# Running maxima of the mLSTM gates: 32 rows at once instead of eight times 4 rows

## The chip, the core and the metric

The kernel runs on one core of a Trainium2 chip. The metric is the device time of one execution in microseconds. Before the change three runs gave 2087.04, 2087.28 and 2087.66 us; their median, 2087.28, is the time before. Engines are named as in the profile: PE is the matrix engine (TensorE), PEld its weight load, DVE the vector engine, ACT the scalar engine, POOL GpSimd, SP the engine whose queue issues most DMAs.

## The reference

One encoder layer over two sequences of 512 tokens (`x_prompt`, `x_sample`) with 1024 channels, in float32: a half-step SwiGLU feed-forward block, a mixing block, a second feed-forward block, a final RMS norm. The mixing block runs attention and a bidirectional mLSTM next to each other on one input projection. The change concerns the mLSTM's stabilisers. Per head (4) and direction (2):

```python
b = jnp.cumsum(lf, axis=-1)                       # lf: log forget gate, within a chunk
D = b[..., :, None] - b[..., None, :] + li[..., None, :]
D = jnp.where(tril, D, -jnp.inf)
inter = b + m[..., None]
m_t = jnp.maximum(inter, jnp.max(D, axis=-1))
...
S_qk = jnp.einsum('bhtd,bhsd->bhts', qc, kc) * jnp.exp(D - m_t[..., None])
...
g = bL[..., None] - b + li
m_new = jnp.maximum(bL + m, jnp.max(g, axis=-1))
```

Since `b_t` does not depend on `s`, the maximum over the row is `b_t` plus a running maximum over `s` of `li_s - b_s`. The second direction is the same on the flipped sequence.

## The kernel before, in words

Tokens are handled in four blocks of 128; the kernel uses these blocks as chunks of the mLSTM, where the reference has 64; the stabilised sums are the same, grouped otherwise. Float32 products are made of three products of split operands (high times high, high times low, low times high), so each projection is a long row of 128 x 128 by 128 x 512 matmuls (L755 for a projection of 128 channels, L739 for one by tokens).

The two sequences go through the generator `mix(s, ...)`, which is advanced in turns: the first sequence (`s` = 0) computes its gates while its own projections run; the second computes them while the output projection of the first (`out_unit`, L1212) is still running, whose squares POOL adds up (L156) and whose result POOL's queue writes (L1213). The order of instructions on each engine is set by a scheduler from priorities, dependences and its own costs; each engine then works through its list in order, and SP through its DMAs in order.

`gates()` turns the gate columns into log gates of shape 128 tokens x 32, where the 32 columns are direction, block and head (`d b h`); one matmul group (L900) makes the cumulative sums `cs`, and `et` (L903) holds the gate exponents, input gate minus cumulative forget gate. What is needed from `et` is its running maximum along the tokens of each block, forward for direction 0 and backward for direction 1, and the exponents as rows in DRAM (`ebuf`). As tokens lie on partitions, the kernel turns `et` first. For each direction:

- four turns on PE (L907), one per block, give 4 rows (heads) of 512 tokens in one PSUM bank;
- DVE copies them to `er` (L909), SP writes them to `ebuf` (L910);
- `mem_max` makes four scans on DVE (L869), one per block, of 4 rows x 128 tokens each;
- for each block PE turns the running maxima back (L874) and the block's last maximum, broadcast over 128 columns (L875); DVE copies both to `st` (L876).

That is 24 turns, 8 scans, 2 copies to `er`, 2 DMAs and 2 copies to `st` per sequence. Around them on PE stand the products of a projection (L755), the turns of the keys (`k_turn`, L847) whose banks ACT empties (L849), and later the turns of the rotated queries (`q_rope`, L960). On DVE stand the sums of squares of the queries (`ssq`, L785), a reciprocal square root (L162 to L192), the rotation of the queries (L796 to L807) and the splitting of weights (L240).

`mem_scales` (L989 to L1000) reads `st` and makes the stabilisers. It is issued in the program after the attention heads, but the scheduler may place it earlier. `mem_rows(h, d)` reads a row of `ebuf`, 512 tokens of one head, broadcast to all 128 partitions (L979), and adds a mask (L983, POOL for the first sequence, DVE for the second); `mem_head` makes the decay weights from them on ACT. PSUM banks for turns come from a pool of two (`PT`), those for scores likewise (`PS`).

Of the kernel before, what the change touches and what calls it, by code (L numbers as in the profile page):

```python
# [8 lines left out]
F32 = mybir.dt.float32  # L9
# [3 lines left out]
ALU = mybir.AluOpType  # L13
AX = mybir.AxisListType
PSUM = bass.MemoryType.PSUM

P = 128
S = 512
# [8 lines left out]
def encoder(ctx, tc, I, outs):  # L27
    nc = tc.nc
    cpool = ctx.enter_context(tc.tile_pool(name="cpool", bufs=1))
    dpool = ctx.enter_context(tc.tile_pool(name="dpool", bufs=1, space=bass.MemoryType.DRAM))  # L30
# [11 lines left out]
    def nm(s):  # L42
        n_id[0] += 1
        return f"{s}_{n_id[0]}"
# [71 lines left out]
    def PT():  # L116
        return pt.tile([P, S], F32, tag="t", name=nm("pst"))
# [8 lines left out]
    ident = cpool.tile([P, P], F32, name="ident")  # L126
# [140 lines left out]
    V_ = nc.vector  # L267
# [394 lines left out]
    HM, DM = 4, 128  # L662
    NEG = -1e30
# [96 lines left out]
    def mix(s, xh, xl, early=None, extra=None, after=None):  # L760
# [8 lines left out]
        def F2(dtype=F32):  # L769
            return T2(dtype, "f2")  # L770
# [81 lines left out]
        def gs(tag):  # L852
            t = small(32, tag)
            return t, t.rearrange("p (d b h) -> p d b h", d=2, b=4)

        cs = small(96, "cs")
        csv = cs.rearrange("p (j d b h) -> p j d b h", j=3, d=2, b=4)
        ebuf = dpool.tile([2, 4, S], F32, name=nm("ebuf"))

        st = spool.tile([P, 4, 2, 4, HM], F32, tag="st", bufs=1, name=nm("st"))  # L860
        n1, bd, en, n2 = [st[:, i] for i in range(4)]

        def mem_max(d, er):

            run = F2()[0:4]
            for b in range(4):
                bs = slice(b * P, (b + 1) * P)
                to, x_ = [t[:, bs] if d == 0 else t[:, bs][:, ::-1] for t in (run, er[0:4])]
                V_.tensor_tensor_scan(to, x_, x_, NEG, op0=ALU.max, op1=ALU.max)  # L869
            p = PT()  # L870
            pv = p[:, 0:32].rearrange("p (i b h) -> p i b h", i=2, b=4)
            for b in range(4):
                end = b * P + (P - 1 if d == 0 else 0)
                nc.tensor.transpose(pv[:, 0, b], run[:, b * P:(b + 1) * P], ident[0:4, 0:4])  # L874
                nc.tensor.transpose(pv[:, 1, b], run[:, end:end + 1].to_broadcast([4, P]), ident[0:4, 0:4])  # L875
            V_.tensor_copy(st[:, 0:2, d], pv)  # L876

        def gates():
            Gb = Gt.rearrange("p (b c) -> p b c", b=4)
# [16 lines left out]
            p = PT()  # L896
# [4 lines left out]
            V_.tensor_copy(cs, p[:, 0:96])  # L901
            et, ev = gs("et")
            V_.tensor_tensor(et, Is, cs[:, 32:64], op=ALU.add)  # L903
            for d in range(2):
                p = PT()
                for b in range(4):
                    nc.tensor.transpose(p[0:4, b * P:(b + 1) * P], ev[:, d, b, :], ident)  # L907
                er = F2()
                V_.tensor_copy(er[0:4], p[0:4])  # L909
                nc.sync.dma_start(ebuf[d], er[0:4])  # L910
                mem_max(d, er)


        Vm = []
# [61 lines left out]
        def mem_rows(h, d):  # L976

            eb = T2(F32, "eb")
            nc.sync.dma_start(eb, ebuf[d, h:h + 1, :].rearrange("a s -> (a s)").partition_broadcast(P))  # L979
            em = T2(F32, "eb")  # L980
            eb3 = eb.rearrange("p (b s) -> p b s", b=4)
            em3 = em.rearrange("p (b s) -> p b s", b=4)
            (G_, V_)[s].tensor_tensor(em3, eb3, tabs[3][:, d].unsqueeze(1).to_broadcast([P, 4, P]), op=ALU.add)  # L983
            return eb3, em3
# [258 lines left out]
    def turn(s, k, bank):  # L1243
        p = bank()
        for b in range(4):
            nc.tensor.transpose(p[:, b * P:(b + 1) * P], raws[s][:, b, k * P:(k + 1) * P], ident)
        return p
# [58 lines left out]
    for k in range(HK_):  # L1306
        x1l, x1u = x1[2 * k % 4], x1[(2 * k + 1) % 4]
        for t, kk, bank, kr in ((x1l, k, PS, orow[3]), (x1u, k + HK_, PT, orow[4])):
            p = turn(1, kk, bank)
# [220 lines left out]
```

## Time and profile before

| | |
|---|---|
| median of three runs | 2087.28 us (2087.04 to 2087.66) |
| profiled execution, its own time | 2087.16 us |
| its span in the trace | 2085.4 us, 27317 instructions |
| PE busy | 2065.5 us, 9520 matmuls and turns |
| DVE busy | 1558.2 us |
| ACT busy | 894.3 us |
| POOL busy | 95.6 us |
| DMA | 454.33 MB, 218 GB/s on average |
| granted clock of PE | 0.998 |

The span is what the trace covers; 1.8 us of the execution lie around it. Rows of the trace name the line of the kernel before, the engine, and the tile written and read (`out<-in`). A row of the timeline gives start, length, engine, line, operation, tiles, shape and count. Since matmuls overlap, a row's length is longer than what the instruction adds to the queue; the distance between starts tells that.

### The profile page before, as it was taken

The page shows a single profiled execution, that of the slowest core. Times are in us where ns is not written, and L with a number is a line of the kernel's source. Part 1 is how long each engine was busy: PE and PEld are TensorE (multiplying, and loading weights), DVE is VectorE, ACT ScalarE, POOL GpSimd, SP SyncE. Part 2 cuts the span into 40 slices and gives each one's busy share as a digit, 9 for nine tenths or more (in the row PEclk, how much of TensorE's full clock was granted, in tenths as well). Part 3 has the DMA queues.
Part 4 walks back from the last instruction along what each step waited for, and adds up shares of the span by engine and source line. Part 5 has one row for each costly group of instructions (what it writes and reads, how often), then busy time and mean ns, then how long its engine had stood idle before and what let it go on. Part 6 is the DMA issues. An engine that isn't in the chain of part 4 may idle for free.

```text
span 2085.4 us, 27317 instructions
## 1 busy us (share of the span) xinstructions
PE 2065.5 (99%) x9520; PEld 1694.8 (81%) x9520; DVE 1558.2 (75%) x2850; ACT 894.3 (43%) x1645; POOL 95.6 (5%) x114
## 2 busy tenths in 40 slices
PE   8999999999999999999999999999999999999998
PEld 6888888888888777888878788888888888888887
DVE  7888888786797897675577645545888888795797
ACT  6544444443234566463344443323544444442222
POOL 1000000001003000100120000002000000000010
PEclk9999999999999999999999999999999999999999
DMA  8655555699766655777675345677656555599853
GB/s 279 204 173 193 192 172 182 205 342 359 259 225 242 202 162 172 257 241 270 214 263 180 103 152 182 203 255 245 205 172 212 185 178 182 180 347 346 274 190 116
DMA packets 300857, 454.33 MB, mean 218 GB/s; under 512 B 20048, under 2 KB 170592, under 8 KB 299696
## 3 DMA queue, kind: packets, MB, share of 16 engines
q1 hardware_dynamic: 298848, 447.13, 63.9%
q0 software_dynamic: 1872, 5.46, 0.8%
q8 instruction: 75, 1.23, 0.2%
q14 instruction: 62, 0.51, 0.1%
HBM read 285.63 MB, written 166.89 MB: 217 GB/s over the span
## 4 chain that ended last, share of the span: by engine, by line
PE 94%; DMA 2%; DVE 2%; ACT 1%; issue 0%; SPq 0%; DVEq 0%; ACTq 0%; POOL 0%
PE mm L755 21%; PE pss L333 17%; PE pst L333 11%; PE mm L333 9%; PE mm L589 9%; PE pst L589 4%; PE pss L589 4%; PE mm L739 4%; PE pso L589 3%; PE pso L1039 1%; PE pss L1012 1%; PE pso L739 1%; PE pst L1031 1%; DMA wr<-in_ffn_w_gate_dram 1%; PE pso L1175 1%; PE pst L755 1%
## 5 line engine op out<-in xcount | busy, mean ns | idle before, releaser
L755 PE MATMUL mm<-xh,w 128*128 128x512 f32 x896 | 291.2, 394 | 0.0
L333 PE MATMUL pss<-xc,w 128*128 128x512 f32 x1056 | 256.3, 391 | 0.7 <-DVE t L364 0.7
L333 PE MATMUL mm<-xc,w 128*128 128x512 f32 x1056 | 253.0, 390 | 2.4 <-ACT w L291 1.9
L333 PE MATMUL pst<-xc,w 128*128 128x512 f32 x1056 | 253.7, 389 | 0.0
L333 PEld LDWEIGHTS pss<-xc,w 128*128 128x128 f32 x1056 | 196.9, 188 | 47.9 <-DVE t L364 7.3
L333 PEld LDWEIGHTS mm<-xc,w 128*128 128x128 f32 x1056 | 197.3, 188 | 45.0 <-ACT w L291 2.8
L333 PEld LDWEIGHTS pst<-xc,w 128*128 128x128 f32 x1056 | 198.1, 188 | 41.4 <-ACT t L368 0.2
L755 PEld LDWEIGHTS mm<-xh,w 128*128 128x128 f32 x896 | 167.7, 188 | 33.6
L589 PE MATMUL mm<-rt,w 128*128 128x512 f32 (+1 forms) x819 | 188.4, 384 | 0.0
L755 PE MATMUL mm<-xl,w 128*128 128x512 f32 x448 | 176.7, 394 | 0.0
L589 PEld LDWEIGHTS mm<-rt,w 128*128 128x128 f32 x819 | 151.3, 188 | 29.8
L291 ACT ACTIVATE w<-t 128x512 fp32r<-128x512 f32 x176 | 106.9, 627 | 139.1 <-issue 55.2
L292 DVE TENSOR_TENSOR w<-t,w 128x512 fp32r<-128x512 f32 x176 | 118.2, 688 | 54.2 <-ACT w L291 52.3
L333 PE MATMUL pss<-xc,f 128*128 128x512 f32 x528 | 126.9, 389 | 0.0
L333 PEld LDWEIGHTS pss<-xc,f 128*128 128x128 f32 x528 | 99.1, 188 | 20.6
L657 ACT ACTIVATE w<-wr 128x512 fp32r<-128x512 f32 x72 | 45.1, 632 | 138.3 <-PE pso L589 70.8
L657 ACT ACTIVATE w<-t 128x512 fp32r<-128x512 f32 x82 | 51.8, 632 | 107.6 <-PE pst L589 62.4
L755 PEld LDWEIGHTS mm<-xl,w 128*128 128x128 f32 x448 | 84.3, 188 | 16.6
L589 PE MATMUL pst<-rt,w 128*128 128x512 f32 x396 | 93.7, 389 | 0.0
L589 PE MATMUL pss<-rt,w 128*128 128x512 f32 x396 | 93.7, 389 | 0.0
L239 ACT ACTIVATE w<-wr 128x1024 fp32r<-128x1024 f32 (+1 forms) x56 | 57.2, 1028 | 71.3 <-PE mm L755 29.8
L589 PEld LDWEIGHTS pss<-rt,w 128*128 128x128 f32 x396 | 74.3, 188 | 15.4
(341 smaller groups left out, 3657.8 us busy)
## 6 DMA issues: line engine op xcount, KB each, us to landing
rt<-rbuf SPq DMA_DIRECT2D x154, 512.0 KB, 5.7
wpark<-w SPq DMA_DIRECT2D x104, 512.0 KB, 3.5
w<-wpark SPq DMA_DIRECT2D x104, 512.0 KB, 4.6
wr<-in_ffn_w_gate_dram SPq DMA_DIRECT2D x62, 512.0 KB, 5.3
rbuf<-tab SPq DMA_DIRECT2D x102, 256.0 KB, 3.8
wr<-in_ffn_w_up_dram SPq DMA_DIRECT2D x44, 512.0 KB, 4.5
rbuf<-f SPq DMA_DIRECT2D x72, 256.0 KB, 3.9
wr<-in_w_in_dram SPq DMA_DIRECT2D x36, 512.0 KB, 6.0
```

Source lines behind the costliest of these rows:

```text
L239: pin(nc.scalar.activation(hi, raw, AF.Copy))
L291: pin(nc.scalar.activation(t[:, 0], src, AF.Copy))
L292: pin(V_.tensor_tensor(t[:, 1], src, f(t[:, 0]), op=ALU.subtract))
L333: nc.tensor.matmul(p, a[:, k, :], xt[:, b, k, :], start=(first and k == 0 and i == 0), stop=(k == HK_ - 1 and i == 2), skip_group_check=True)
L589: nc.tensor.matmul(p, u[:, a, d * P:(d + 1) * P], r[:, b, ts], start=(first and q == 0 and k == 0), stop=(q == len(us) - 1 and k == 2), sk ...
L657: nc.scalar.activation(hi, src, AF.Copy)
L739: nc.tensor.matmul(p[b][:, :N], a[:, k, bs], w_[:, kl, :], start=(k == 0 and i == 0), stop=(k == KD - 1 and i == 2))
L755: nc.tensor.matmul(p, a[:, k, :], b, start=(k == 0 and i == 0), stop=(k == n - 1 and i == 2))
L1012: nc.tensor.matmul(p, qT[:, h, b * P:(b + 1) * P], kv[:, hk * 2 + j, :], start=(j == 0), stop=(j == 1))
L1031: nc.tensor.transpose(p[:, b * P:(b + 1) * P], Ps[b][:, kb * P:(kb + 1) * P], ident)
L1039: nc.tensor.matmul(po, Vst[:, kv_, hk, :], w, start=(kv_ == 0 and i == 0), stop=(kv_ == 3 and i == 1))
L1175: nc.tensor.matmul(po, vm[:, a, t, hs_], b, start=(t == 0 and n == 0), stop=(t == 3 and n == 2))
```

## The change

All 32 rows (direction, block, head) are handled together. One turn takes `et` as a whole (128 x 32) to 32 rows of 128 tokens. One copy and one DMA bring them to `er` and `ebuf`, which now is laid out as direction, block, head, token. One scan runs backward over all 32 rows and then a second forward over the first 16, direction 0, overwriting them. The block's last maximum is the maximum of the row, made by one reduction (`top`). Two turns, of the running maxima and of `top` broadcast over 128 columns, and one copy fill `st`. Per sequence these are 3 turns, 2 scans, 1 reduction, 2 copies and 1 DMA. `mem_rows` reads the row of a head as four pieces of 128 tokens, one for each block, because in the new layout the blocks of a head lie apart.

```diff
--- before.py
+++ after.py
@@ -855,25 +855,9 @@
 
         cs = small(96, "cs")
         csv = cs.rearrange("p (j d b h) -> p j d b h", j=3, d=2, b=4)
-        ebuf = dpool.tile([2, 4, S], F32, name=nm("ebuf"))
-
+        ebuf = dpool.tile([2, 4, HM, P], F32, name=nm("ebuf"))
         st = spool.tile([P, 4, 2, 4, HM], F32, tag="st", bufs=1, name=nm("st"))
         n1, bd, en, n2 = [st[:, i] for i in range(4)]
-
-        def mem_max(d, er):
-
-            run = F2()[0:4]
-            for b in range(4):
-                bs = slice(b * P, (b + 1) * P)
-                to, x_ = [t[:, bs] if d == 0 else t[:, bs][:, ::-1] for t in (run, er[0:4])]
-                V_.tensor_tensor_scan(to, x_, x_, NEG, op0=ALU.max, op1=ALU.max)
-            p = PT()
-            pv = p[:, 0:32].rearrange("p (i b h) -> p i b h", i=2, b=4)
-            for b in range(4):
-                end = b * P + (P - 1 if d == 0 else 0)
-                nc.tensor.transpose(pv[:, 0, b], run[:, b * P:(b + 1) * P], ident[0:4, 0:4])
-                nc.tensor.transpose(pv[:, 1, b], run[:, end:end + 1].to_broadcast([4, P]), ident[0:4, 0:4])
-            V_.tensor_copy(st[:, 0:2, d], pv)
 
         def gates():
             Gb = Gt.rearrange("p (b c) -> p b c", b=4)
@@ -901,14 +885,20 @@
             V_.tensor_copy(cs, p[:, 0:96])
             et, ev = gs("et")
             V_.tensor_tensor(et, Is, cs[:, 32:64], op=ALU.add)
-            for d in range(2):
-                p = PT()
-                for b in range(4):
-                    nc.tensor.transpose(p[0:4, b * P:(b + 1) * P], ev[:, d, b, :], ident)
-                er = F2()
-                V_.tensor_copy(er[0:4], p[0:4])
-                nc.sync.dma_start(ebuf[d], er[0:4])
-                mem_max(d, er)
+            p = PT()
+            nc.tensor.transpose(p[0:32, 0:P], et, ident)
+            rows = F2()[0:32]
+            er, run = rows[:, 0:P], rows[:, P:2 * P]
+            V_.tensor_copy(er, p[0:32, 0:P])
+            nc.sync.dma_start(ebuf.rearrange("d b h s -> (d b h) s"), er)
+            V_.tensor_tensor_scan(run[:, ::-1], er[:, ::-1], er[:, ::-1], NEG, op0=ALU.max, op1=ALU.max)
+            V_.tensor_tensor_scan(run[0:16], er[0:16], er[0:16], NEG, op0=ALU.max, op1=ALU.max)
+            top = rows[:, 2 * P:2 * P + 1]
+            V_.tensor_reduce(top, er, axis=AX.X, op=ALU.max)
+            p = PT()
+            nc.tensor.transpose(p[:, 0:32], run, ident[0:32, 0:32])
+            nc.tensor.transpose(p[:, 32:64], top.to_broadcast([32, P]), ident[0:32, 0:32])
+            V_.tensor_copy(st[:, 0:2], p[:, 0:64].rearrange("p (i d b h) -> p i d b h", i=2, d=2, b=4))
 
 
         Vm = []
@@ -976,9 +966,9 @@
         def mem_rows(h, d):
 
             eb = T2(F32, "eb")
-            nc.sync.dma_start(eb, ebuf[d, h:h + 1, :].rearrange("a s -> (a s)").partition_broadcast(P))
+            eb3 = eb.rearrange("p (b s) -> p b s", b=4)
+            nc.sync.dma_start(eb3, ebuf[d, :, h, :].partition_broadcast(P))
             em = T2(F32, "eb")
-            eb3 = eb.rearrange("p (b s) -> p b s", b=4)
             em3 = em.rearrange("p (b s) -> p b s", b=4)
             (G_, V_)[s].tensor_tensor(em3, eb3, tabs[3][:, d].unsqueeze(1).to_broadcast([P, 4, P]), op=ALU.add)
             return eb3, em3
```

## The prediction

> **What bounds the kernel now.** I read the page first, then the waits of TensorE (PE), the windows around the two gate computations, and the timelines of both.
>
> ```profile
> span 2085.4 us, 27317 instructions
> PE 2065.5 (99%) x9520; PEld 1694.8 (81%) x9520; DVE 1558.2 (75%) x2850; ACT 894.3 (43%) x1645; POOL 95.6 (5%) x114
> PE 94%; DMA 2%; DVE 2%; ACT 1%; issue 0%; SPq 0%; DVEq 0%; ACTq 0%; POOL 0%
> PE pst L874 <- DVE f L869: 1.0, 1, 1.0
> ```
>
> PE is busy for 2065.5 of 2085.4 us and makes 94% of the chain that ended last (third line). The last line is from PE's waits (total us, times, longest): beyond the start of the program, the one wait of a microsecond belongs to the code that changes, a transpose (L874) that waits for a running maximum (L869). So the kernel ends when PE has worked through its queue, and every PE instruction taken out should show in the time unless it uncovers a wait.
>
> ```profile
> 690.00:706.00 16.00, 15.98 (x93) 12.09 (x92) 10.99 (x38) 7.52 (x14) 0.00 (x0) 1.00 0.38 103
> 706.00:720.00 14.00, 14.00 (x75) 11.53 (x74) 13.94 (x31) 8.34 (x17) 0.00 (x0) 1.00 0.69 225
> 1066.00:1080.00 14.00, 14.00 (x77) 11.44 (x76) 13.78 (x33) 8.33 (x18) 1.10 (x2) 1.00 0.89 296
> 1080.00:1110.00 30.00, 30.00 (x138) 24.78 (x137) 11.62 (x14) 7.71 (x13) 8.69 (x9) 1.00 0.95 343
> ```
>
> Columns: stretch, length, busy time of PE, PEld, DVE, ACT, POOL, granted clock, DMA share, GB/s. The first sequence's gates lie in 690 to 706: PE is never free there, the clock is full, POOL is idle. Just behind the gates of either sequence DVE (VectorE) is as full as PE (13.94 and 13.78 of 14), so DVE work that goes is useful too, but alone it would not show.
>
> **The turns that go.** First sequence: from the first turn of `et` to the steady product stream behind the gates.
>
> ```profile
> 694.65 0.60 PE L907 MATMUL pst<-ident,et 128*4 128x128 f32 x4
> 705.09 0.70 PE L755 MATMUL mm<-xh,w 128*128 128x512 f32 x2
> ...
> L755 PE MATMUL mm<-xh,w 128*128 128x512 f32 x14 | 4.8, 412 | 0.0
> L755 PE MATMUL mm<-xl,w 128*128 128x512 f32 x7 | 3.0, 433 | 0.0
> L847 PE MATMUL pst<-ident,qT 128*128 128x128 f32 x16 | 2.8, 286 | 0.0
> ...
> 703.55 0.87 PE pst L847 x8
> 705.33 3.90 PE mm L755 x17
> ```
>
> Two timeline rows, then the groups between them, then two pieces of the chain. Durations of single matmuls overlap, so I price by the chain: an undisturbed product takes 3.90/17 = 0.229 us, a full turn 0.87/8 = 0.109. The stretch is 705.09 - 694.65 = 10.44 us and holds 21 products and 16 other turns: 10.44 - 21 x 0.229 - 16 x 0.109 = 3.89 us are the 24 turns of the gates. Eight of these are L907, 0.87 us by the price of a full turn; the other eight pairs (L874 with L875) then cost 3.02/8 = 0.38 us each: narrow turns between wide products slow their neighbours.
>
> Second sequence, likewise:
>
> ```profile
> 1055.52 0.60 PE L907 MATMUL pst<-ident,et 128*4 128x128 f32 x4
> 1057.80 0.39 PE L755 MATMUL mm<-mh,w 128*128 128x512 f32 x1
> 1059.16 0.19 PE L874 MATMUL pst<-ident,f 4*128 4x4 f32 x1 [0.97 <-DVE f L869]
> 1066.42 0.38 PE L847 MATMUL pst<-ident,qT 128*128 128x128 f32 x2
> ...
> L755 PE MATMUL mm<-mh,w 128*128 128x512 f32 x15 | 5.2, 411 | 0.0
> L755 PE MATMUL mm<-ml,w 128*128 128x512 f32 x7 | 2.8, 402 | 0.0
> L847 PE MATMUL pst<-ident,qT 128*128 128x128 f32 x12 | 2.1, 286 | 0.0
> ```
>
> 10.90 - 22 x 0.229 - 12 x 0.109 = 4.55 us. Of that, 1059.16 - 1057.80 - 0.23 = 1.13 us is the wait for the scan; 3.42 us are turns, 0.32 a pair.
>
> The changed kernel has one L907-like turn and one pair. Turns of 32 rows do not occur in this trace; the bounds are a full turn, 0.11, and the pair of 4 rows, 0.38; I take 0.11 plus one pair, 0.49 and 0.43. Removed: 3.40 + 2.99 = 6.39 us. If the three cost as little as full turns, 0.2 more goes.
>
> **What PE waits for then, first sequence.** The order listing of the changed kernel puts eight products between the turn of `et` and the turn of the running maxima, where ten stood. Eight products end at about 694.65 + 0.11 + 8 x 0.229 = 696.6. On DVE the chain is copy, a `ssq` reduction that the scheduler put between, scan, reduction, scan.
>
> ```profile
> 693.59 0.26 DVE L901 COPY cs<-pst 128x96 f32<-128x96 f32 x1 [1.21 <-PE pst L900]
> 694.53 0.68 DVE L785 TENSOR_REDUCE ssq<-t 128x8 f32<-128x512 f32 x1
> 696.49 0.40 DVE L869 TENSOR_TENSOR_SCAN f<-f 4x128 f32<-4x128 f32 x1
> 696.82 0.14 DVE L162 TENSOR_SCALAR rs<-ssq 128x32 f32<-128x32 f32 x1
> ```
>
> The copy of 128 columns is priced by L901 (96 columns, 0.26): 0.29, 0.2 until the next can start. A scan has 0.40 and lets the next start after 0.33; 32 partitions instead of 4 with the same 128 columns should cost the same (eight 128-column scans become two, so at most this doubles to 0.8 each; nothing shows that). The reduction of 128 columns is a quarter of L785, 0.2 to 0.3. One turn lasts 0.27 (0.60 for four, less three starts of 0.109), so the copy starts at 694.96, and 0.22 + 0.60 + 0.33 + 0.20 + 0.40 brings the last scan's end to 696.7. PE follows a scan by some 0.15 (worked out from the next rows): 696.85, a new wait of 0.2. At double scans it is 0.9. Behind the DVE copy, which now waits for a turn that has just been issued, stand the `ssq` reduction and the rest of DVE's queue; this idles DVE 0.35 us, covered by its 5 us of free time in 690 to 706.
>
> **The second sequence: a shared wait.**
>
> ```profile
> L869 DVE TENSOR_TENSOR_SCAN f<-f x16: 385/404/1489, 696.5 to 1062.7; 4x128 f32<-4x128 f32 x16
> 1056.32 0.67 DVE L909 COPY f<-pst 4x512 f32<-4x512 f32 x1
> 1056.92 0.67 DVE L796 TENSOR_TENSOR t<-t,rs 128x512 f32<-128x512 f32 x1
> 1057.52 2.43 DVE L869 TENSOR_TENSOR_SCAN f<-f 4x128 f32<-4x128 f32 x4
> 1056.71 0.54 POOL L1213 DMA_DIRECT2D x2buf<-f  x1 [6.23 <-DVE f L1212]
> 1057.27 1.47 POOL L156 TENSOR_TENSOR R<-R,t 128x512 f32<-128x512 f32 x1
> ```
>
> One scan of 16 took 1489 ns instead of 404: the first of the second sequence, from 1057.52 to 1059.01. POOL's add ran from 1057.27 to 1058.74; the scan finished 0.27 after it. That is what PE waited for: it went on at 1059.16, 0.15 behind the scan. The Trainium skill (SBUF — State Buffer, "Who interferes with whom") says that a DVE instruction with two SBUF inputs and a GpSimd instruction that reads SBUF exclude each other for the whole instruction, and that a reduction does not take part; by that rule, with which this row agrees, the second of the two new scans can be caught as the first was.
>
> In the changed order the copy (now L909, 0.60 from its start to that of L796) takes 0.22, so L796 starts at about 1056.54 and the first scan 0.60 later at 1057.14, 0.13 before POOL's add, which follows POOL's transfer issue of 1056.71. Either the scan is first, POOL starts at 1057.5 and the second scan waits until about 1058.9 and ends at 1059.15; or the first scan is caught, ends at 1059.0 as now, and the second at 1059.6. PE gets on at 1059.3 or 1059.75. Its ten products end at about 1058.0 in both kernels. So the wait is 1.3 or 1.75, I take 1.45, where it was 1.13: 0.3 lost. At best, if no scan is caught, it is 0.2 and 0.9 is won; at worst a second add of POOL follows, 1.3 more. Behind a caught scan stand the steps of the query rotation on DVE; PE asks for their turns some 3.5 us later (16 turns and six products), which covers it.
>
> **What else moves.** The `kv` turns (L847) now stand in one block, each needing a bank that ACT or DVE has just emptied; PE may stand 0.15 us per sequence there, 0.3 in all. The small steps of `mem_scales` move ahead of the query rotation in the first sequence; DVE has 14 instructions fewer in all, 2 x (2 x 0.68 + 8 x 0.40) = 9.1 us of copies and scans give way to about 2.8, so the rotation still starts earlier by as much as PE does. On ACT the exponential of `mem_scales` now stands before the fourth `kv` copy and waits for DVE; the bank that this holds is asked for only some 29 products later. On SP two `ebuf` writes become one; in the second sequence a weight load that stood behind the later of them is issued earlier. The sixteen `mem_rows` loads read four pieces of 512 bytes per partition instead of one of 2 KB: taken at nothing, with their price among the rivals.
>
> **Sum**, against the profiled execution's own time of 2087.16 us (span 2085.4 and 1.8 around it; the three runs' median is 2087.28): -6.39 + 0.2 + 0.3 + 0.3 = -5.6, so 2081.6 us. The bounds make it 2081.0 (cheap turns, the short wait, no stand at the `kv` turns) to 2083.2 (double scans, the long wait, 0.6 at the `kv` turns). A change of 0.2%, 4.2 us, is about what a measurement of this kernel can tell from no change.
>
> **Rivals.**
>
> A. No scan meets POOL: the wait of 1.13 shrinks to 0.2 instead of growing to 1.45, 1.25 better than the sum, 2080.3 us. For it: the scan leads POOL's add by an estimated 0.13 us; against it: the second scan starts well inside the add. 16%.
>
> B. Part of the gain is lost in the score stage. From about 730 us on, the order listing shows scores, turns and products of the first sequence interleaved anew, and DVE is full there (13.94 of 14 before it). If PE waits for bank after bank on DVE, I price it at half of what is removed from the first sequence's DVE and PE queues, 2 to 3 us: 2084.1. Against it: DVE's work shrinks by as much as PE's. 15%.
>
> C. The loads of `mem_rows` land late, and the kernel is slower.
>
> ```profile
> box<-ebuf SPq DMA_DIRECT2D x16, 256.0 KB, 4.6
>   DVE box L983: 12.8, 6
> wr<-in_w_in_dram SPq DMA_DIRECT2D x36, 512.0 KB, 6.0
> 1107.52 0.69 DVE L983 TENSOR_TENSOR box<-box,tab 128x512 f32<-128x512 f32 x1 [2.77 <-DMA box<-ebuf]
> 1109.50 0.69 DVE L937 TENSOR_TENSOR f<-mm,R 128x512 f32<-128x512 f32 x1 [0.69 <-PE mm L755]
> ```
>
> In the second sequence DVE itself waits for such a load (2.77 us at 1107.52), with the query split and the score maxima queued behind it; 0.69 us of slack stand at L937. Eight loads of that sequence feed DVE; if the six for which DVE waited (second row: 12.8 us in six waits) land x later, PE loses up to 6 (x - 0.7). It outweighs the gain by 0.2% from 6 (x - 0.7) = 5.6 + 4.2, x = 2.3 us; at 3 us later the time is 2081.6 + 13.8 = 2095. Against it: a weight load of twice the bytes, also in pieces of 512 bytes (128 columns), lands in 6.0, so x should be below 1.4. The Trainium skill (DMA: Bandwidth & Descriptors, "Specifications") puts the least piece for full rate at 512 bytes, which these just meet; by that rule x is near nothing. 5%.
>
> D. PE's gain is given back at the next supply limit: in 1080 to 1110 DMA stands at 0.95 and 343 GB/s, and weights that land when they land hold PE at the old time. 2086.5. Against it: PE is busy for 30.00 of the 30 us there, so no weight came late. 6%.
>
> The forecast keeps 58%. That the edit does not do what it says is no rival: the order listing shows 3 gate turns a sequence for 24, and DVE's 14 instructions fewer.
>
> **Chances.** Faster by over 0.2%: forecast and A, 74%. Within 0.2% (above 2083.0): B and D, 21%. Slower: C, 5%. The range 2079.6 to 2084.4 holds the forecast, A and most of B.
>
> **What would show it.** Right: L907, L874 and L875 replaced by three turns a sequence; PE's waits show one wait of 1.2 to 1.8 us for a scan near 1054 (both stretches lie about 3 us earlier by then) and about 0.2 near 697; one long scan; the span 5 to 6 us shorter, nearly all of it before 1070. Wrong: a `box<-ebuf` landing above 7 us with DVE waiting behind it, PE waits for `asm` or `pss` after 720, or a turn of 32 rows that costs several tenths.

## The result and the profile after

The changed kernel takes 2084.39 us (median of 20 runs, 2081.34 to 2086.01), the kernel before 2087.56 us in the runs beside it (median of 20). The ratio is 0.9982, with a 95% interval of 0.9975 to 0.9989: 3.8 us faster. In three later comparisons, beside the experiments, it was 0.9974 [0.9965, 0.9984], 0.9975 [0.9965, 0.9985] and 0.9976 [0.9967, 0.9985], 5.0 to 5.4 us. (The ratio is estimated from all the runs and is not the quotient of the two medians; the medians themselves lie 3.2 us apart in the first comparison and 5.1, 4.2 and 5.2 us in the later ones.) The forecast was 5.6 us, 2081.6, with a range up to 2084.4; the first median lies at that upper end, inside by 0.01 us, which is luck, the three later ones (2083.19, 2084.06, 2082.98) well inside. Against the bound of 0.2% the first comparison, 0.18%, falls just short, and the later ones, 0.24 to 0.26%, beyond. The profiled execution took 2082.11 us against 2087.16 before: 5.05 less.

So there are two things to explain: where 5 us came from, and why the first set of runs shows less of them than the profile. Two lines of the page of the changed kernel, then TensorE's waits that are new in it (engine, bank and line that waited, what it waited for; us in total, times, longest):

```profile
span 2080.3 us, 27215 instructions
...
PE 2060.4 (99%) x9478; PEld 1691.4 (81%) x9478; DVE 1551.1 (75%) x2836; ACT 894.6 (43%) x1645; POOL 97.7 (5%) x114
```

```profile
PE pst L899 <- DVE f L895: 0.9, 1, 0.9
...
PE pst L1021 <- DVE t L658: 0.4, 1, 0.4
...
PE pst L950 <- DVE t L658: 0.2, 1, 0.2
```

TensorE is as full as before. The gate stage of the first sequence, on TensorE (start, duration, line, operation):

```profile
694.11 0.27 PE L889 MATMUL pst<-ident,et 128*32 128x128 f32 x1
694.14 0.71 PE L755 MATMUL mm<-xh,w 128*128 128x512 f32 x2
...
695.62 0.63 PE L755 MATMUL mm<-xh,w 128*128 128x512 f32 x2
696.28 0.21 PE L899 MATMUL pst<-ident,f 32*128 32x32 f32 x1
696.33 0.22 PE L900 MATMUL pst<-ident,f 32*128 32x32 f32 x1
696.48 0.66 PE L847 MATMUL pst<-ident,qT 128*128 128x128 f32 x4
696.89 0.48 PE L755 MATMUL mm<-xl,w 128*128 128x512 f32 x1
697.21 1.27 PE L847 MATMUL pst<-ident,qT 128*128 128x128 f32 x8
```

and beside it on DVE:

```profile
695.22 0.40 DVE L894 TENSOR_TENSOR_SCAN f<-f 32x128 f32<-32x128 f32 x1
695.55 0.25 DVE L897 TENSOR_REDUCE f<-f 32x1 f32<-32x128 f32 x1
695.73 0.40 DVE L895 TENSOR_TENSOR_SCAN f<-f 16x128 f32<-16x128 f32 x1
```

Read from one start to the next, the three new turns cost 0.03, 0.05 and 0.15: 0.23 us in all. A product beside turns is slowed as well: the one between the key turns (L847) takes 0.32 from its start to theirs (696.89 to 697.21), where an undisturbed one takes 0.229. A scan of 32 rows takes the 0.40 us that one of 4 rows took. The second scan ends at 696.13 and TensorE goes on 0.15 later, at 696.28; the products in front of it were issued out at about 696.08 (695.62 + 2 x 0.229), so it stood 0.2 us, of which the waits view says nothing.

The second sequence, on DVE, GpSimd and TensorE:

```profile
1053.90 0.40 DVE L894 TENSOR_TENSOR_SCAN f<-f 32x128 f32<-32x128 f32 x1
1054.24 0.25 DVE L897 TENSOR_REDUCE f<-f 32x1 f32<-32x128 f32 x1
1054.41 1.25 DVE L895 TENSOR_TENSOR_SCAN f<-f 16x128 f32<-16x128 f32 x1
```

```profile
1054.05 1.33 POOL L156 TENSOR_TENSOR R<-R,t 128x512 f32<-128x512 f32 x1
```

```profile
1054.26 0.63 PE L755 MATMUL mm<-mh,w 128*128 128x512 f32 x2
1055.81 0.21 PE L899 MATMUL pst<-ident,f 32*128 32x32 f32 x1 [0.92 <-DVE f L895]
```

The first scan is ahead of GpSimd's addition and takes 0.40; the second starts inside it, takes 1.25 and ends at 1055.66, 0.28 after the addition. TensorE's two products were out at 1054.72; it stood 1.09 us. (The figure in brackets counts from the modelled end of the product before it; counted the same way as the 1.13 of before, it is 1.09.)

Where the time went can be told stage by stage from the start of the same TensorE instruction in both traces. The table gives the difference to the kernel before, in us, with what the two executions already differ by at the first product of the mixing block (L739, 657.21 before) taken out; that difference, in the bottom row, arises almost whole in the first 100 us, in waits for loads of the inputs and of the first weights, ahead of all that the change touches. The kernels named in the other columns follow below.

| TensorE instruction (time before) | after | again | again2 | again3 | psum | psume | dvrow | all3 |
|---|---|---|---|---|---|---|---|---|
| first score product, 1st sequence (717.58) | -3.01 | -3.01 | -2.97 | -3.02 | -3.23 | -3.20 | -2.98 | -3.20 |
| last score product, 1st sequence (806.08) | -2.70 | -3.08 | -2.38 | -2.62 | -3.37 | -3.43 | -3.65 | -4.02 |
| last cumulative sum, 2nd sequence (1050.28) | -2.73 | -3.07 | -2.25 | -2.69 | -3.11 | -3.29 | -3.65 | -4.03 |
| first score product, 2nd sequence (1109.30) | -5.27 | -5.57 | -4.77 | -5.22 | -6.63 | -6.81 | -5.85 | -7.27 |
| 33rd score product, 2nd sequence (1143.18) | -5.27 | -5.55 | -4.16 | -5.19 | -5.65 | -6.79 | -5.81 | -7.24 |
| last turn of the memory heads, L1167 (1325.83) | -5.04 | -5.35 | -3.97 | -4.99 | -5.43 | -6.47 | -5.77 | -7.26 |
| a product of the second feed-forward block (1617.29) | -5.04 | -5.05 | -2.23 | -4.87 | -4.84 | -5.46 | -5.79 | -5.33 |
| end (2085.40) | -4.57 | -4.62 | -1.79 | -4.39 | -4.36 | -4.99 | -5.69 | -5.22 |
| taken out: difference at 657.21 | -0.49 | -0.36 | -1.32 | -0.77 | +0.50 | -0.28 | +0.30 | -0.72 |

In all four executions of the changed kernel the first gate stage gives 2.97 to 3.02 us and the second (row 4 less row 3) 2.50 to 2.54. What differs between them lies elsewhere: 0 to 0.6 us lost in the score stage, 0.6 near 1106 in one of them, 1.7 between 1326 and 1617 in the same one. All four lose 0.43 to 0.48 more between 1617 and the end. Most of that is one wait, first in the changed kernel, then in the kernel before:

```profile
2057.84 0.66 PE L1409 MATMUL pss<-ident,xs 128*128 128x128 f32 x4 [0.63 <-DVE t L1420]
```

```profile
2063.00 0.66 PE L1419 MATMUL pss<-ident,xs 128*128 128x128 f32 x4 [0.28 <-DVE t L1430]
```

It is 0.35 us longer in every execution of the changed kernel; the traces do not show why.

### The profile page after: what moved, and what is told of

Same layout as the page of the kernel before. It is cut to its first block, busy times and chain, and to the rows that moved or that the text cites. A ratio compares the mean times of both kernels' runs of the same rounds, so it can differ in the third digit from the quotient of the medians.

```text
span 2080.3 us, 27215 instructions
## 1 busy us (share of the span) xinstructions
PE 2060.4 (99%) x9478; PEld 1691.4 (81%) x9478; DVE 1551.1 (75%) x2836; ACT 894.6 (43%) x1645; POOL 97.7 (5%) x114
## 3 DMA queue, kind: packets, MB, share of 16 engines
q0 software_dynamic: 1872, 5.46, 0.8%
## 4 chain that ended last, share of the span: by engine, by line
PE 95%; DVE 3%; DMA 1%; ACT 1%; issue 0%; SPq 0%; DVEq 0%; ACTq 0%
PE mm L755 20%; PE pss L333 17%; PE pst L333 11%; PE mm L333 10%; PE mm L589 9%; PE pst L589 4%; PE pss L589 4%; PE mm L739 4%; PE pso L589 3%; PE pso L1029 1%; PE pss L1002 1%; PE pso L739 1%; PE pst L1021 1%; PE pso L1165 1%; PE pst L755 1%; PE pss L755 1%
## 5 line engine op out<-in xcount | busy, mean ns | idle before, releaser
L755 PE MATMUL mm<-xh,w 128*128 128x512 f32 x896 | 290.4, 394 | 0.0
L755 PEld LDWEIGHTS mm<-xh,w 128*128 128x128 f32 x896 | 167.7, 188 | 33.5
L755 PE MATMUL mm<-xl,w 128*128 128x512 f32 x448 | 176.2, 393 | 0.0
L755 PEld LDWEIGHTS mm<-xl,w 128*128 128x128 f32 x448 | 84.2, 188 | 16.6
```

The lines of the kernel that those rows point to most:

```text
L755: nc.tensor.matmul(p, a[:, k, :], b, start=(k == 0 and i == 0), stop=(k == n - 1 and i == 2))
```

## The experiments

Times of the kernels are medians; each group of runs shares the runs of the kernel before on its chip (2088.24, 2088.24 and 2088.15 us for the three groups). The theory at the outset: the time is what TensorE issues, plus its waits in the two gate stages. The rivals: the loads of 512 bytes, the order in the score stage, and, for the gain, the shorter chain on DVE.

**again** is the changed kernel, unaltered.

> The changed kernel once more, nothing altered. Its profiled execution took 2082.11 us, but the median of its runs was 2084.39, and they lie between 2081.3 and 2086.0 where those of the kernel before lie within some 2 us. Theory 1 (the time is what TensorE issues, plus the waits of the gate stage): the second profile shows the same two gate stages, about 2.6 and 2.5 us shorter than before, and what differs between executions lies outside of them. Rival 2 (the loads of mem_rows in pieces of 512 bytes): an execution that takes 2084 or more shows waits of TensorE or of DVE for box from ebuf that last longer than the 3.2 and 2.5 us of the first profile, and TensorE idle behind them by 1 to 3 us. Rival 3 (the order in the score stage): the difference lies between 725 and 800 us, as in the first profile, where 0.6 us was lost.

Measured: 2083.19 us (10 runs, 2081.66 to 2084.66); the profiled one 2082.19. Its gate stages are those of the first profile to 0.04 us. In the score stage it lost nothing, where the first lost 0.3. It was not a late execution, so it could not tell the rivals apart.

**rows512** is the kernel before with the new layout of `ebuf` alone:

```diff
-        ebuf = dpool.tile([2, 4, S], F32, name=nm("ebuf"))
+        ebuf = dpool.tile([2, 4, HM, P], F32, name=nm("ebuf"))
-                nc.sync.dma_start(ebuf[d], er[0:4])
+                nc.sync.dma_start(ebuf[d].rearrange("b h s -> h b s"), er[0:4].rearrange("h (b s) -> h b s", b=4))
-            nc.sync.dma_start(eb, ebuf[d, h:h + 1, :].rearrange("a s -> (a s)").partition_broadcast(P))
+            nc.sync.dma_start(eb3, ebuf[d, :, h, :].partition_broadcast(P))
```

> The kernel before with the new layout of ebuf alone: gate turns and maxima as before, two writes of ebuf, and the sixteen mem_rows loads read four pieces of 512 bytes per partition in place of one of 2 KB. The order of the instructions on every engine is that of the kernel before. Theory 1: same as before, 0.9998 to 1.0004; the load lands in about 4.8 us (median) where it was 4.6, and TensorE does not wait for it. Rival 2 (the small pieces cost time or make the executions differ): slower by 1 to 3 us (ratio 1.0005 to 1.0015), or runs that spread over 4 us instead of 2.

Measured: 2088.64 us (11 runs), ratio 1.0003 [0.9995, 1.0012]. The view of the loads' line, the same kernel's waits of TensorE below it:

```profile
DMA to landing us min/median/max: 3.2/5.0/7.6
```

```profile
PE pst L874 <- DVE f L869: 1.0, 1, 1.0
...
PE pst L1031 <- DVE t L658: 0.6, 2, 0.4
```

The median landing went from 4.6 to 5.0 us, x = 0.4 in the terms of rival C, where 2.3 was needed to turn the sign. The time is the same within its interval, and the runs spread no more than those of the kernel before on that chip (2086.2 to 2092.7). The pieces of 512 bytes cost nothing that shows in the time. The Trainium skill (DMA: Bandwidth & Descriptors, "Specifications") puts the least piece for full rate at 512 bytes; the unchanged time agrees, and no run here has smaller pieces. The second row of waits is of interest for later: this kernel, with the old gate stage and the old order, also stood 0.4 us in the score stage, where the profile of before shows no such wait.

**psum** lets both scans read one of their two equal inputs from the accumulator:

```diff
+            pr = p[0:32, 0:P]
-            V_.tensor_tensor_scan(run[:, ::-1], er[:, ::-1], er[:, ::-1], NEG, op0=ALU.max, op1=ALU.max)
-            V_.tensor_tensor_scan(run[0:16], er[0:16], er[0:16], NEG, op0=ALU.max, op1=ALU.max)
+            V_.tensor_tensor_scan(run[:, ::-1], pr[:, ::-1], er[:, ::-1], NEG, op0=ALU.max, op1=ALU.max)
+            V_.tensor_tensor_scan(run[0:16], pr[0:16], er[0:16], NEG, op0=ALU.max, op1=ALU.max)
```

> The changed kernel, but both scans take the first of their two equal inputs from the accumulator tile that the turn of et left, and the second from er as before, so that a scan reads one input from SBUF and not two. The results are the same. If it is the two SBUF inputs that make a scan and an addition of GpSimd exclude each other: the second scan of the second sequence takes 0.4 us in place of 1.25, and TensorE's wait of 0.9 us before the turn of the running maxima shrinks to 0.1 to 0.3; the kernel is 0.7 to 0.9 us faster than the changed one (ratio to before 0.9978 if the changed one is at 0.9982). If the second scan was long for another reason (a wait for something else of the same length), it stays at 1.2 and the time does not change. Rival: a scan that reads an accumulator is slower by itself (0.6 instead of 0.4), which would take back 0.2 us.

The second scan of the second sequence, GpSimd's addition beside it, and TensorE:

```profile
1055.02 0.40 DVE L896 TENSOR_TENSOR_SCAN f<-pst,f 16x128 f32<-16x128 f32 x1
1055.35 1.16 DVE L800 TENSOR_TENSOR t<-t,tab 128x512 f32<-128x512 f32 x1
```

```profile
1054.65 1.29 POOL L156 TENSOR_TENSOR R<-R,t 128x512 f32<-128x512 f32 x1
```

```profile
1055.32 0.39 PE L755 MATMUL mm<-ml,w 128*128 128x512 f32 x1
1055.64 0.24 PE L900 MATMUL pst<-ident,f 32*128 32x32 f32 x1
```

With one input in SBUF the scan runs through GpSimd's addition at its full 0.40 us; the next instruction with two SBUF inputs, L800, is now the one that waits (1.16 us; 0.65 in the changed kernel). TensorE's wait is gone, and the second gate stage gives 3.52 us instead of 2.50 to 2.54 (table). That settles the lock for the scan: it is the second SBUF input. The Trainium skill (SBUF — State Buffer, "Who interferes with whom") states it so, that a DVE instruction with at most one SBUF input, outside the 2-port perf modes, does not contend with GpSimd; this run agrees, for a scan too.

But the kernel's median fell by only 0.6 us (2082.63 in 7 runs, against 2083.19 of again), which the runs do not tell from nothing (both ratios to the kernel before are 0.9974), and in the profile nothing is left of the gain after 1143 us (-6.63 becomes -5.65). DVE and TensorE of this kernel show why:

```profile
1099.78 0.69 DVE L974 TENSOR_TENSOR box<-box,tab 128x512 f32<-128x512 f32 x1 [5.14 <-DMA box<-ebuf]
```

```profile
1106.53 0.73 PE L1003 MATMUL pss<-kv,qT 128*128 128x512 f32 x2 [0.71 <-ACT t L1008]
```

DVE stood 5.14 us for the first load of `mem_rows` of the second sequence; behind that addition stand the query split and the score maxima, ACT's exponential follows those, and TensorE waits 0.71 us for the bank that the exponential frees. The same load in the kernel before, on SP's queue:

```profile
1077.46 1.65 SPq L979 DMA_DIRECT2D box<-ebuf  x1
```

and in the changed kernel, with DVE's two waits for it and its follower:

```profile
1080.86 7.36 SPq L254 DMA_DIRECT2D w<-wpark  x6
1088.32 0.40 SPq L970 DMA_DIRECT2D box<-ebuf  x1
```

```profile
1098.20 0.69 DVE L973 TENSOR_TENSOR box<-box,tab 128x512 f32<-128x512 f32 x1 [3.19 <-DMA box<-ebuf]
...
1102.03 0.69 DVE L973 TENSOR_TENSOR box<-box,tab 128x512 f32<-128x512 f32 x1 [2.54 <-DMA box<-ebuf]
```

The changed order puts the load behind six weight loads, 11 us later than before, and DVE goes on 9.9 us after its issue. The changed kernel just stays free of it; a little earlier on TensorE, or a little later in landing, and it costs.

**narrow** gives the changed kernel 21 narrow turns more per sequence:

```diff
             nc.tensor.transpose(p[0:32, 0:P], et, ident)
+            for i in range(7):
+                nc.tensor.transpose(p[0:4, (1 + i % 3) * P:(2 + i % 3) * P], et[:, 4 * i:4 * i + 4], ident)
...
+            for i in range(7):
+                nc.tensor.transpose(p[:, 64 + 8 * i:68 + 8 * i], run[0:4], ident[0:4, 0:4])
+                nc.tensor.transpose(p[:, 68 + 8 * i:72 + 8 * i], top[0:4].to_broadcast([4, P]), ident[0:4, 0:4])
```

> The changed kernel with 21 narrow turns more per sequence, whose results nobody uses: seven turns of four columns of et to 4 rows, and seven pairs of turns of 4 rows, all into free places of the same accumulator tiles. Copies, scans and loads stay as in the changed kernel, so that TensorE alone has about the number of turns of the kernel before (24 a sequence) and DVE has not. Theory 1 (the gain is TensorE's turns): priced from the kernel before, 7 x 0.11 + 7 x 0.38 = 3.4 us and 7 x 0.11 + 7 x 0.32 = 3.0 us are added, of which the second sequence can put the seven turns of et, 0.8, in front of its wait at no gain; the time is 5.6 to 6.4 us above that of the changed kernel, slower than before by up to 2 us. Rival 4 (the gain came from the shorter chain of copies and scans on DVE, and narrow turns lie in the shadow of weights being loaded): less than 1.5 us above the changed kernel.

Measured: 2087.70 us (11 runs), 4.5 above again; in the profiles 6.0 (2088.20 against 2082.19). The ratio to the kernel before is 0.9992 [0.9983, 1.0001]. DVE keeps the short chain here and the gain is gone, so it did not come from that chain, and the turns do not lie in the shadow of weight loads: rival 4 falls. But the price of a turn was wrong too:

```profile
694.62 0.93 PE L891 MATMUL pst<-ident,et 128*4 128x128 f32 x7
695.30 0.71 PE L755 MATMUL mm<-xh,w 128*128 128x512 f32 x2
...
1060.34 0.20 PE L904 MATMUL pst<-ident,f 4*128 4x4 f32 x1
1060.40 0.19 PE L905 MATMUL pst<-ident,f 4*128 4x4 f32 x1
...
1061.13 0.19 PE L905 MATMUL pst<-ident,f 4*128 4x4 f32 x1
1061.25 1.46 PE L847 MATMUL pst<-ident,qT 128*128 128x128 f32 x8
```

Seven turns of `et` take 0.68 us from start to start, and seven pairs 0.91 (1060.34 to 1061.25): 0.13 a pair, 1.6 us per sequence, half of what was expected. The rest of the 6 us came mostly as waits around them (the scheduler's order of other work moved too, so not all of it need be the turns' doing): TensorE stood 1.4 us once in the score stage (next row), and in the second sequence the sixteen turns of L847 take 2.68 us instead of 1.80 from start to start. The expected total came out in the profile, though not in the medians, and from partly wrong terms.

```profile
PE pst L1026 <- DVE t L658: 1.6, 2, 1.4
```

**again2** is the changed kernel once more, in a second group of runs.

> The changed kernel a third time, unaltered, as the mark for the other three on the same chip and to look at one more execution. Theory 2, formed after the run psum: in the second sequence the first load of mem_rows now stands behind six weight loads on SP (issued at 1088.3, landed at 1098.2, DVE waited 3.2 us for it); TensorE loses nothing as long as it lands by about 1099, and loses what it is later by (0.7 us in psum, where it landed at 1099.8). An execution above 2083.5 should then show TensorE waiting for pss in 1100 to 1112, and one below should not. Theory 1 alone: the executions differ at the start (the first products, up to 1 us) and nowhere else.

Measured: 2084.06 us (9 runs, 2082.48 to 2085.42), and this profiled execution was a late one, 2084.06. Between the first gate stage and the tail TensorE waited in three places that cost it more than in the kernel before; ACT's row belongs to the last:

```profile
751.99 0.66 PE L1021 MATMUL pst<-ident,t 128*128 128x128 f32 x4 [0.63 <-DVE t L658]
```

```profile
1106.21 0.73 PE L1002 MATMUL pss<-kv,qT 128*128 128x512 f32 x2 [0.34 <-ACT t L1007]
```

```profile
1484.85 3.06 PE L333 MATMUL mm<-xc,w 128*128 128x512 f32 x12 [1.32 <-ACT f L341]
```

```profile
1479.85 0.60 ACT L341 ACTIVATE f<-mm 128x512 f32<-128x512 f32 x1 [3.10 <-DMA kept<-f]
```

The second is the late load, as theory 2 says, though with 0.3 to 0.6 us it is not the largest. The third is new: in the second feed-forward block an eviction of ACT waits 3.10 us for a store (`kept`) to land, and TensorE loses 1.3 us behind it. Theory 1's "differ at the start and nowhere else" is wrong; theory 2 names one place of three.

**early** moves the first two loads of `mem_rows` of the second sequence ahead of the six weight loads, by priority; only SP's order and the place of two DVE additions change:

```diff
+            with shifted(-860 if s == 1 and h == 0 else 0): nc.sync.dma_start(eb3, ebuf[d, :, h, :].partition_broadcast(P))
```

> The changed kernel, but the first two mem_rows loads of the second sequence are issued ahead of the six weight loads, at about 1074 instead of 1088 and 1094, and DVE's two additions that read them stand some 10 us earlier on DVE; TensorE's, ScalarE's and GpSimd's orders are those of the changed kernel. Theory 2: DVE's waits of 3.2 and 2.5 us for box near 1098 are gone; a good execution takes what the changed kernel's profiled one takes (2082), since that lost nothing on TensorE, and the late ones go: a median 0.5 to 1.5 us lower than the changed kernel's beside it, and a narrower spread. Theory 1 alone: the same median and the same spread. Against both: if the two loads delay the weights behind them, slower by up to 1 us.

**psume** is psum with the same line.

> Both edits together: the scans read one input from the accumulator, and the first two mem_rows loads of the second sequence are issued ahead of the six weight loads. Theory 2: the 1.0 us that psum won before 1100 and lost again between 1103 and 1137 is now kept: 0.9 to 1.1 us below the changed kernel in the profile of equal start (about 2081), and the fastest of all; the wait of 0.71 for pss is gone. Theory 1 without the load's landing: as psum, no gain over it.

Measured: early 2082.90 us (7 runs, 2081.95 to 2084.63), 1.2 below again2; psume 2082.39 (5 runs, 2081.89 to 2082.74), 1.7 below it, and the narrowest of that group. All but one of early's runs lie among those of again2 (2082.48 to 2085.42) and they spread about as widely, 2.7 against 2.9 us, so the narrower spread that was expected did not come and its gain is not clear of noise; of psume's five, three lie below all nine of again2. In psume's profile the wait near 1106 is gone, and the table shows the second gate stage's 3.52 us kept at 1143 us (-6.81, then -6.79), where psum lost 0.98. At the end of the profile 0.4 of this is left against the first two of the changed kernel (-4.99 against -4.57 and -4.62), where 0.9 to 1.1 was expected: 1.0 us went between 1326 and 1617. Early's profile ends 1.2 us below again2's; it has no wait near 1106 (none was lost in the first profile either), and loses 1.1 us between 1241 and 1326 and 0.8 at the store of `kept`. SP and DVE in early:

```profile
1073.73 0.76 SPq L970 DMA_DIRECT2D box<-ebuf  x1
```

```profile
1086.39 0.69 DVE L973 TENSOR_TENSOR box<-box,tab 128x512 f32<-128x512 f32 x1 [4.63 <-DMA box<-ebuf]
```

DVE still waits for the second load, but 15 us sooner, where nothing queues behind it that TensorE needs. That the late load takes up a gain made ahead of it is shown by psum against psume; how much of the spread it makes in the changed kernel these few runs do not settle.

**rows2k** is the changed kernel with the old layout of `ebuf`: two writes, and loads of 2 KB.

```diff
+        ebuf = dpool.tile([2, 4, S], F32, name=nm("ebuf"))
+            for d in range(2):
+                nc.sync.dma_start(ebuf[d].rearrange("h (b s) -> b h s", b=4), er[d * 16:(d + 1) * 16])
+            nc.sync.dma_start(eb, ebuf[d, h:h + 1, :].rearrange("a s -> (a s)").partition_broadcast(P))
```

> The changed kernel with the old layout of ebuf: two loads write it, and mem_rows reads 2 KB in one piece per partition again. Gate turns, scans and reduction are those of the changed kernel; the order of the second sequence shifts a little. Theory 2 (the place of the load in SP's queue, not its pieces): its first landing in the second sequence is as late as in the changed kernel where it stands behind the same six weight loads, 8 to 11 us, and the time is that of the changed kernel within 0.05%. Rival 2 (the pieces of 512 bytes): the loads land 1 to 3 us sooner, and the median is 1 to 2 us below the changed kernel's.

Measured: 2082.45 us (6 runs, 2081.76 to 2084.01), 1.6 below again2, which is rival 2's number. But the test is spoilt: the order shifted, and the first load is issued at 1076.7, ahead of the weight loads, as in early. The second still stands behind them (issued 1093.67, DVE goes on at 1100.84, 7.2 us later; in the four executions of the changed kernel, with 512-byte pieces, 7.2 to 9.3 us). One landing at the low end of that range does not tell what the pieces cost, and the gain of rows2k is no evidence against them; the 0.4 us of rows512 is the price that was measured with the order unchanged.

The third group asks for the loss in the score stage. In the changed kernel's first profile, at 749 us, on GpSimd and DVE, and TensorE behind:

```profile
748.89 1.29 POOL L973 TENSOR_TENSOR box<-box,tab 128x512 f32<-128x512 f32 x1 [0.30 <-DMA box<-ebuf]
```

```profile
749.08 1.39 DVE L1009 TENSOR_SCALAR t<-t,asm 128x512 f32<-128x512 f32 x1
```

```profile
752.55 0.66 PE L1021 MATMUL pst<-ident,t 128*128 128x128 f32 x4 [0.42 <-DVE t L658]
```

A scaling whose median is 0.48 us takes 1.39 and ends 0.29 after GpSimd's addition; DVE is busy for 15.18 of the 16 us from 740 to 756, and TensorE waits 0.42 us for a split of DVE a few instructions later. The same scaling in again and in again2:

```profile
749.22 0.48 DVE L1009 TENSOR_SCALAR t<-t,asm 128x512 f32<-128x512 f32 x1
```

```profile
748.30 1.61 DVE L1009 TENSOR_SCALAR t<-t,asm 128x512 f32<-128x512 f32 x1
```

In again GpSimd's addition started after the scaling, at 749.44, and TensorE did not wait; in again2 TensorE waited 0.63 us. GpSimd's second addition starts when its load has landed (the brackets of the first row above), so which of the two is first hangs on that landing.

**again3** is the changed kernel; **dvrow** lets DVE make the first two of these additions of each sequence, which in the first sequence takes them from GpSimd (in the second they are DVE's already); **all3** is psume with that line.

```diff
-            (G_, V_)[s].tensor_tensor(em3, eb3, tabs[3][:, d].unsqueeze(1).to_broadcast([P, 4, P]), op=ALU.add)
+            (V_ if h == 0 else (G_, V_)[s]).tensor_tensor(em3, eb3, tabs[3][:, d].unsqueeze(1).to_broadcast([P, 4, P]), op=ALU.add)
```

> The changed kernel once more, as the mark on the same chip for the two others. Theory 2: the score stage of the first sequence (728 to 800 us) loses between 0 and 0.8 us against the kernel before, depending on which DVE instruction is running when GpSimd starts its two additions of mem_rows near 747; the rest of its difference lies at the start, near 1106 and near 1484.

> The changed kernel, but the first two additions of mem_rows of the first sequence (128 x 512 each, 1.3 us on GpSimd) run on DVE instead of GpSimd; the scheduler moves some products and DVE steps between 750 and 800 us. Theory 2 (the 0.2 to 0.7 us lost in the score stage come from DVE instructions that GpSimd's additions hold up, such as the 1.39 us scaling at 749): TensorE no longer waits for t there and the stage loses 0 to 0.2 us in every execution; the median falls by 0.2 to 0.5 us. Rival (the stage is bound by DVE's own work): two more additions of 0.69 us on DVE make TensorE wait longer, and the median rises by 0.5 to 1.2 us.

> Three edits on the changed kernel: scans with one input from the accumulator, the first two mem_rows loads of the second sequence ahead of the weight loads, and the first two mem_rows additions of the first sequence on DVE. Theory 2: as the two first edits together, about 1.0 us below the changed kernel's profile at an equal start, and 0.2 to 0.5 us more in the median; spread of its runs below 2 us apart from the start. Rival as in dvrow: 0.5 to 1.2 us slower than the two first edits alone.

Measured: again3 2082.98 us (10 runs), dvrow 2081.24 (6 runs, 2079.69 to 2081.86), all3 2081.17 (5 runs, 2080.16 to 2081.22). Again3 lost 0.4 us in the score stage (its scaling took 1.38, and TensorE waited 0.41 behind it), dvrow none: it won 0.67 there (table, -2.98 to -3.65). So the loss was GpSimd's additions holding up DVE, and two more additions on DVE cost TensorE nothing that shows. What dvrow won beyond the loss can also come from the order, which the scheduler changed there. The median fell by 1.7 us, more than the 0.2 to 0.5 expected; 1.0 of it is the stage and 0.35 the wait near 2058, which in dvrow, all3 and rows2k is as short as in the kernel before; the remainder is not explained by these traces. All3's mixing block is 7.26 us shorter than before's, 1.9 to 3.3 better than the changed kernel's four; then it lost 1.9 us in the second feed-forward block:

```profile
PE mm L333 <- ACT f L341: 1.3, 1, 1.3
```

Its ratio to the kernel before is 0.9967 [0.9955, 0.9980], dvrow's 0.9968 [0.9956, 0.9980], the changed kernel's beside them 0.9976 [0.9967, 0.9985]. By medians these two are the fastest here, 1.7 and 1.8 us under the changed kernel beside them: all five runs of all3 and four of the six of dvrow lie below the ten of again3 (2081.36 to 2083.91), though the intervals of the ratios overlap.

## Why the prediction was right, and where it was not

- **What bounds the kernel.** Right: TensorE's queue. The gain is TensorE's: with 21 narrow turns a sequence put back it was gone, about half by the turns themselves and most of the rest by waits around them (narrow).
- **The first gate stage.** Forecast 3.40 removed, 0.2 and 0.15 given back: 3.05. Measured 2.97 to 3.02. The terms were off in both directions, and that they cancel is luck. The 24 old turns were worth about 3.3, not 3.89: 2.57 us from start to start (0.89, 0.68 and 1.00 for L907, L874, L875), and 0.7 in the products beside them (L755, from the last cumulative sum to the first score product, 18.09 us before and 17.55 after, of which 0.2 is the new wait). The remainder that was read as 3.89 also held the products that the key turns slow, and those stay (0.32 instead of 0.229 beside L847 after the change). The three new ones cost 0.23, not 0.49: the pair was priced by the pair of 4 rows, 0.38, and the one pair of 32 rows costs 0.20. The stand at the `kv` turns, 0.15, did not come; the sixteen took 1.80 us instead of 1.91.
- **The new wait there.** Forecast 0.2, measured 0.20, by the step as written (last scan's end plus 0.15 against the end of eight products), though all of it happened half a microsecond sooner.
- **The second gate stage.** Forecast 2.99 less 0.3 less 0.15, so 2.54; measured 2.50 to 2.54. The first of the two branches came: the first scan led, the second was caught. The wait was 1.09 instead of the 1.45 taken (1.3 in that branch), the three turns cost 0.23 instead of 0.43, and the old turns were again worth less than the 3.42 put down: 2.58 us from start to start (0.89, 0.65 and 1.04), and 0.32 in the sixteen key turns, which took 2.11 before and 1.79 after. Here too the sum fits because its errors cancel. That it is the two SBUF inputs was shown by psum.
- **Rival A** (no scan meets GpSimd, 1.25 better): did not happen, and psum, which makes it happen, is worth 1.0 us at that place.
- **Rival B** (part lost in the score stage, 2 to 3 us, 15%): it happened, small: 0 to 0.6 us in four executions. The mechanism was another than the one named; not the changed order but GpSimd's additions of `mem_rows`, which fall on an almost full DVE. The four executions show it (a scaling of 1.39, 0.48, 1.61 and 1.38 us, and a wait of 0.42, none, 0.63 and 0.41), dvrow confirms it, and rows512, with the order of before, stood there too, behind a split of 1.61 us beside the same addition.
- **Rival C** (512-byte pieces): x is 0.4 in the median of the landings, the sum unchanged (rows512). But the step "taken at nothing" missed what matters about these loads: the change moved the first of them, in SP's queue, behind six weight loads. The prediction followed DVE's and ACT's queues there and of SP's only the `ebuf` writes and one weight load. It costs 0 to 0.6 us in the changed kernel, and in psum 1.0, all that was gained ahead of it. The prediction's own sign of being wrong, a landing above 7 us with DVE waiting behind it, was there in all four executions (8.4 to 10.1 us, DVE waiting 1.9 to 3.6), and TensorE lost time in one of them; the kernel before had such a landing too (8.0 us, the load of 1099.5 for which DVE waits 2.77), so the sign was set too low to tell.
- **Rival D** (given back at DMA's limit in 1080 to 1110): not as priced, 4.9; the late load in that very stretch is a small form of it.
- **The size in the median.** The sum was made against the profile and gave 5.6; the profile gave 5.05, the comparisons 3.8 and three times 5.0 to 5.4. What is short of 5.6 are the losses outside the gate stages (score stage, the load near 1106, the store near 1484) and 0.45 us in the tail, none of which the sum held; the cause of the tail's share is open, and only the first two are the change's neighbours. The first set's median is 0.3 to 1.4 above the later ones. That set left only one trace, so which of the places made it so stays open.

## What to carry to other kernels

Price a small instruction by where it stands: here a pair of turns of 4 rows cost 0.13 us in a block of its like (narrow), and before 0.21 from start to start with slowed products beside it, so a price taken from one place did not hold in another. When a change removes work from the engine that sets the time, follow every queue's order, SP's above all, to the next point where a load or a shared port is late; the executions of this kernel differed at such points, and the 1.0 us that psum gained ahead of one was kept past it only when the load moved too (psume). And if a DVE instruction with two SBUF inputs meets GpSimd on the path, read one input from the accumulator (psum) or move GpSimd's work (dvrow). A scaling of one tensor by a column of scalars was held up as well, so it is worth looking for in the same way.

## What was not expected of the hardware

- A scan over 128 columns takes 0.40 us on 4, 16 or 32 partitions, and the same with one input in PSUM; caught behind a GpSimd addition, with both inputs in SBUF, it ends 0.27 (before) or 0.28 us (after) after it.
- Turns of 4 rows in a block step at 0.06 us, turns of `et` to 4 rows at 0.10, the first of two turns of 32 rows at 0.05 and the one after it at 0.15.
- A load of 256 KB from `ebuf`, in pieces of 512 bytes, landed in 3.2 us at the least and in 8.4 to 11.6 behind six weight loads (changed kernel and psum); the pieces themselves made 0.4 us in the median (rows512).
- A scaling of 128 x 512 by a column of scalars, 0.48 us by the median, took 1.38 to 1.61 when GpSimd's addition ran beside it.
- All profiled executions run the same work up to the mixing block, and reach it between 655.89 (again2) and 657.71 us (psum): 1.8 us of difference, nearly all of it from loads in the first 100 us.
